# Retention's values and gates: half of their K blocks by seven products in place of eight

## The chip, the cores and the metric

The kernel runs on one core of one Trainium2 chip. The metric is the device time of one execution in microseconds (us). Engines are named as in the profile: PE is TensorE's matmuls, PEld its weight loads, DVE VectorE, ACT ScalarE, POOL GpSimd, SP SyncE, which issues most loads.

## The reference

Two layers of a decoder trunk on 256 positions of width 2048, in float32. Layer 0 mixes with a gated delta rule and latent attention, layer 1 with retention; each layer then has a gated feed-forward network (FFN) with a short convolution and a gated per-layer embedding. The change touches the retention mixer, cut here to what matters:

```python
def odd_mixer(hn, cos, sin, w_in, ret_norm, w_out):
    q, k, v, g = split_cols(hn @ w_in, L1_SPLITS)      # 8 heads: q, k 256 wide, v, g 512 wide
    y = retention(q, k, v, cos, sin, ret_norm)
    return (jax.nn.silu(g) * y) @ w_out

h = h + odd_mixer(rmsnorm(h, attn_norm), ...)
h = h + conv_ffn(rmsnorm(h, ffn_norm), ...)
h = h + ple_term(h, p[1], ...)
```

`retention` rotates q and k, forms per head the decayed scores of q and k, multiplies them by v, and normalises each row of 512 by its mean and variance.

## The kernel before

**Arithmetic.** The 256 rows are two halves of 128 (`NH` = 2). Every float32 operand x is split into hi, a cast to fp32r on ACT, and lo = x - hi on DVE. A product is three matmuls: hi·hi, lo(activation)·hi(weight) and hi·lo(weight). Weights come by SP as 1 MB loads into four `raw` buffers; `cut` (L187, L188) splits them in two pieces of 128x1024 each, into four buffers for hi and four for lo. One load, its two splits and their matmuls are a *unit*: two generator steps for the hi matmuls, one for the lo ones (`UNIT` = 3).

**The two forms of a projection.** `gemm_b` (L266 hi, L271 lo) gives the transposed result, with weights as the stationary operand: 16 matmuls of 512 columns and 16 of 256. `gemm_a` (L295, L296 hi, L301 lo) gives rows of positions: 24 matmuls of 512 columns for four K blocks and 512 output columns.

**Products by sevens.** The FFN's down projection takes part of its K blocks as 2x2 blocks of 512x512 by 512x512 and forms them by seven products instead of eight (`seven`, L442, L443 hi, L447 lo: 12 matmuls each). The activations' four combinations come from `Forms` (L380 to L388). On the weights' side a running total of blocks is kept in two buffers: SP loads the first block into it (`begin`, L407), and POOL's queue issues loads that add the next block to it in memory (`plus`, L411). One operand, t3, is a sum that DVE makes (L467). The seven results are added to h on DVE. The FFN issues one product after each main unit.

**A retention head** (`ret_head`) runs its stages one behind the other: q and k by `gemm_b`, two units each, with rotation on DVE; the values by `gemm_a` over all 16 K blocks, four units, with the scores (L1232) behind the first unit's hi matmuls; then the split of the values (vh L1242 on ACT, vl L1243 on DVE), and the gates by `gemm_a`, four units, with the attention (`mm3`, L244, L245, L247: nine matmuls) behind the first unit's hi matmuls. Statistics (L1258 to L1262, with a reciprocal root on POOL, L156) and normalising (L1265) follow on DVE. `finish` (silu L1272, gate L1273, then the transposes L315 and their split L319, L320 in `gained`) is put off by `later`: it runs as the step of a queue that `turn` serves after each generator step, here the next head's. After heads 3, 5 and 7 the output projection takes up what is ready (`ret_out`, `proj_add`).

**Order.** A list scheduler of the framework orders each engine's instructions from the program's order and its own estimates; each engine then runs its own list strictly in order, and buffers come free as their last readers pass.

Of the kernel before, what the change touches and what calls it, by code (L numbers as in the profile page):

```python
# [13 lines left out]
F32 = mybir.dt.float32  # L14
# [70 lines left out]
def trunk(ctx: ExitStack, tc: tile.TileContext, a: dict):  # L85
# [237 lines left out]

    class Norm:
        def __init__(self, gain):
            self.gain = gain
            self.tiles = []
            self.ssq = small(8)
            self.r = None

        def feed(self, c):
            self.tiles += gained([h[i][c] for i in range(NH)], self.gain + c * 4)
            self.squares(c)
# [12 lines left out]
        def diagonal(self):  # L346
            self.dg = t1((P, 2, P))
            V.tensor_tensor(self.dg, bcm(ident, 2), bcs(self.r, P), op=ALU.mult)
# [20 lines left out]
    class Forms:  # L369
# [6 lines left out]
        def add(self, y0, y1):  # L376
# [4 lines left out]
            V.scalar_tensor_tensor(s2, s1, -1.0, a11, op0=ALU.mult, op1=ALU.subtract)  # L381
            V.tensor_sub(s3, a11, a21)
            V.scalar_tensor_tensor(s4, a12, -1.0, s2, op0=ALU.mult, op1=ALU.subtract)
            hi = [t2((P, 2, 2, P), F32R) for _ in range(2)]
            lo = [t2((P, 2, 2, P), F32R) for _ in range(2)]
            for j in range(2):
                A.copy(hi[j], f[j])
                V.tensor_sub(lo[j], f[j], hi[j].bitcast(F32))  # L388
            self.hi.append(hi)
            self.lo.append(lo)  # L390

        def left(self, n):
            def at(q, k):
                return self.hi[q][n // 2][:, n % 2, k], self.lo[q][n // 2][:, n % 2, k]
            return at

    class Quads:


        def __init__(self, w, r0, c, total):  # L400
            self.blocks = w[r0 : r0 + 8 * P, c * 512 : (c + 2) * 512].rearrange("(q h k p) (e n) -> q h e p k n", q=2, h=2, k=2, e=2)
            self.c = c
            self.total = total

        def put(self, dst, hh, e):
            for q in range(2):
                nc.sync.dma_start(dst[q], self.blocks[q, hh, e])  # L407

        def plus(self, hh, e):
            for q in range(2):  # L410
                G.dma_start(self.total[q], self.blocks[q, hh, e], accum_op=ALU.add)  # L411
# [10 lines left out]
    def running():  # L422
        return [xtile().bitcast(F32).rearrange("p a b c -> p a (b c)") for _ in range(2)]

    def seven(ready, tiles, forms, then):

        quads = ready.popleft()
        c, run_t, fresh, plus = quads.c, quads.total, quads.fresh, quads.plus

        def x(half, i):  # L430
            def at(q, k):
                return xl(tiles, 4 * q + 2 * half + k, i)
            return at

        def product(o, left, right, start):
            los = []
            for q in range(2):
                hi, lo = cut(right[q], 2, 512)
                los.append(lo)
                for k in range(2):  # L440
                    l = left(q, k)
                    T.matmul(o, l[0], hi[k], start=start and q + k == 0, stop=False, skip_group_check=True)  # L442
                    last_mm[0] = T.matmul(o, l[1], hi[k], start=False, stop=False, skip_group_check=True)  # L443
                yield
            for q in range(2):
                for k in range(2):
                    last_mm[0] = T.matmul(o, left(q, k)[0], los[q][k], start=False, stop=q + k == 2, skip_group_check=True)  # L447
            yield

        h11, h12, h21, h22 = h[0][c], h[0][c + 1], h[1][c], h[1][c + 1]  # L450
        acc = pb()
        yield from product(acc, x(0, 0), run_t, True)
        V.tensor_add(h11, h11, acc)
        plus(0, 1)
        one = pb()
        yield from product(one, x(1, 0), fresh(1, 0), True)
        V.tensor_add(h11, h11, one)
        two = pb()
        yield from product(two, forms.left(0), run_t, True)
        V.tensor_sub(h22, h22, two)  # L460
        plus(1, 1)
        b22 = fresh(1, 1)
        yield from product(two, forms.left(3), b22, False)
        V.tensor_sub(h12, h12, two)
        t3 = fresh(0, 1)
        for q in range(2):
            V.tensor_add(t3[q], t3[q], b22[q])  # L467
        yield from product(acc, forms.left(1), run_t, False)
        V.tensor_sub(h12, h12, acc)
        plus(1, 0)  # L470
        yield from product(acc, forms.left(2), t3, False)
        V.tensor_sub(h22, h22, acc)
        yield from product(acc, x(1, 1), run_t, False)
        then()
        V.tensor_add(h21, h21, acc)
# [576 lines left out]
    def ffn(l, nf, nxt, aside=None):  # L1052
# [44 lines left out]
        jobs = deque((g0, c) for g0, cols in by_seven.items() for c in cols)  # L1097
        ready = deque()
        total = []

        def following():
            if not total:
                total.extend(running())
            if jobs:
                g0, c = jobs.popleft()
                ready.append(Quads(w_dn, g0 * P, c, total))
                ready[-1].begin()

        def down(g0, g1, tiles, forms):
            fast = chain(*[seven(ready, tiles, forms, following) for _ in by_seven[g0]])  # L1110
# [13 lines left out]
        for n, (g0, g1) in enumerate(groups):  # L1124
# [3 lines left out]
            for _ in range(LAG * UNIT):  # L1128
                next(going)
            if prev is None:  # L1130
                following()
                run(going)
            else:
                behind_it = down(*prev)
                share = sum(7 if c in by_seven[prev[0]] else 2 for c in range(0, CG, 2)) + 2 * (len(by_seven[prev[0]]) == 1)
                share /= 2 * (g1 - g0) - LAG
                owed = 0.0
                for m, _ in enumerate(going, 1):
                    if m % UNIT:
                        continue  # L1140
                    owed += share
                    while owed >= 1.0:
                        owed -= 1.0
                        for _ in range(UNIT):
                            next(behind_it, None)
                run(behind_it)
# [49 lines left out]
    n1 = Norm(C_NORM["l1_attn_norm"])  # L1196
# [21 lines left out]
    def ret_head(i8, tail):  # L1218
        gq = ret_rope(256 * i8)
        if tail is not None:  # L1220
            later(lambda: None, tail)
        q = run(gq)
        k = run(ret_rope(2048 + 256 * i8))
        dec = t2((P, 384))
        nc.scalar.dma_start(dec, a["decay"][:, 384 * i8 : 384 * (i8 + 1)])
        gv = gemm_a(w1, 0, KB, 4096 + 512 * i8, 512, X1)
        for _ in range(2):
            next(gv)
        ps = pb()
# [7 lines left out]
        ps = run(gv)  # L1237
        v = []
        for i in range(NH):
            vh, vl = t2(dt=F32R), t2(dt=F32R)  # L1240
            r = n1.r[:, i : i + 1]
            A.activation(vh, ps[:, i], AF.Copy, scale=r)  # L1242
            V.scalar_tensor_tensor(vl, ps[:, i], r, vh.bitcast(F32), op0=ALU.mult, op1=ALU.subtract)  # L1243
            v.append((vh, vl))
        gg = gemm_a(w1, 0, KB, 8192 + 512 * i8, 512, X1)
        for _ in range(2):
            next(gg)
        ps = [pb() for _ in range(NH)]
# [4 lines left out]
        mm3(ps[0], [(pl(0), v[0])], True, True)  # L1253
        mm3(ps[1], [(pl(P), v[0]), (pl(S), v[1])], True, True)
        ys = []
        for i in range(NH):
            st = small(6)
            V.bn_stats(st, ps[i])  # L1258
            mv = small(2)
            V.bn_aggr(mv, st)  # L1260
            rs = small(2)
            V.tensor_scalar(rs[:, 0:1], mv[:, 1:2], EPS, None, op0=ALU.add)  # L1262
            rsqrt(rs[:, 1:2], rs[:, 0:1], 1)
            y = t2()
            V.tensor_scalar(y, ps[i], mv[:, 0:1], rs[:, 1:2], op0=ALU.subtract, op1=ALU.mult)  # L1265
            ys.append(y)
        ps = run(gg)

        def finish():
            for i in range(NH):  # L1270
                t = t2()
                A.activation(t, ps[:, i], AF.Silu, scale=n1.r[:, i : i + 1])  # L1272
                V.tensor_mul(ys[i], ys[i], t)  # L1273
            ret_x.extend(gained(ys, C_RN + 4 * i8))

        return finish
# [6 lines left out]
    tail = None  # L1283
# [4 lines left out]
    later(lambda: None, tail)  # L1288
# [204 lines left out]
```

## Time and profile before

| | before |
|---|---|
| three runs | 2855.48, 2854.13, 2855.10 us (median 2855.1) |
| profiled execution | 2853.73 us, its span 2852.0 us |
| granted TensorE clock | 0.999 |
| retention stage | about 1300 to 2060 us of the span |
| loads from memory | 580.94 MB, 204 GB/s over the span |

In the profile's groups, a line such as `L188 DVE ...` gives busy time and mean duration, then the idle time of the engine ahead of it and who ended that. In a timeline a row has its start, its duration, engine, line, operation and tiles; a matmul's listed duration is longer than the step from one start to the next, because they are pipelined, so the step is what counts.

### The profile page before, as it was taken

The numbers are of one execution on the slowest core, as the hardware profiler recorded it, in microseconds if no ns is written. First come the engines' busy times: TensorE is split into PE (matmuls) and PEld (weight loads), VectorE is DVE, ScalarE is ACT, GpSimd is POOL, SyncE is SP. The second block draws the span as 40 slices with busy tenths as digits, with TensorE's granted clock in tenths as the row PEclk, the third lists the DMA queues.
The fourth block names the chain that finished last, engine by engine and source line by source line (L and its number), as shares of the span: only waits on it lengthen the run. The fifth ranks groups of instructions, "written<-read, shape, count | busy, mean of one in ns | idle before, by whom it ended". The sixth has DMA issues, their size and how long they took to land.

```text
span 2852.0 us, 38914 instructions
## 1 busy us (share of the span) xinstructions
PE 2832.8 (99%) x14956; PEld 2440.3 (86%) x14956; DVE 2163.5 (76%) x3016; ACT 1606.0 (56%) x2253; POOL 194.6 (7%) x176
## 2 busy tenths in 40 slices
PE   9999999999999999999999999999999999999998
PEld 9899988888888888888888888888888888888887
DVE  7888867898989898756556565565679899989775
ACT  7666655566666665554444443444556666666554
POOL 0111100011111110000000000000001111111100
PEclk9999999999999999999999999999999999999999
DMA  7444456588888988655555555555559889898854
GB/s 244 131 133 130 131 169 210 187 232 252 244 251 243 255 239 254 189 183 190 182 185 186 188 186 180 192 182 186 193 185 243 254 238 259 236 260 252 242 176 144
DMA packets 422650, 585.57 MB, mean 205 GB/s; under 512 B 12096, under 2 KB 268224, under 8 KB 422464
## 3 DMA queue, kind: packets, MB, share of 16 engines
q1 hardware_dynamic: 389664, 521.66, 55.5%
q0 software_dynamic: 29376, 56.63, 11.8%
q10 hardware_dynamic: 3424, 4.79, 0.5%
q8 instruction: 117, 1.92, 0.3%
q14 instruction: 69, 0.57, 0.1%
HBM read 580.94 MB, written 2.10 MB: 204 GB/s over the span
## 4 chain that ended last, share of the span: by engine, by line
PE 98%; DVE 1%; ACT 1%; DMA 0%; issue 0%; POOL 0%; ACTq 0%; POOLq 0%; DVEq 0%
PE pa L266 30%; PE pa L271 16%; PE pa L301 10%; PE pa L296 10%; PE pa L295 10%; PE pb L443 4%; PE pb L442 4%; PE pb L447 4%; PE pb L735 2%; PE pb L315 1%; PE pb L296 1%; PE pb L295 1%; PE pb L301 1%; PE pa L932 1%; PE pb L741 0%; PE pb L1232 0%
## 5 line engine op out<-in xcount | busy, mean ns | idle before, releaser
L188 DVE TENSOR_TENSOR lo<-raw,hi 128x1024 fp32r<-128x1024 f32 (+3 forms) x1104 | 1153.7, 1069 | 473.7 <-ACT hi L187 399.9
L187 ACT CAST hi<-raw 128x1024 fp32r<-128x1024 f32 (+3 forms) x1104 | 971.2, 927 | 816.6 <-PE pa L296 328.9
L266 PE MATMUL pa<-xg,hi 128*128 128x512 f32 x3840 | 925.5, 391 | 0.0
L266 PEld LDWEIGHTS pa<-xg,hi 128*128 128x128 f32 x3840 | 711.4, 188 | 142.2 <-DVE xg L320 0.3
L271 PEld LDWEIGHTS pa<-xg,lo 128*128 128x128 f32 x3840 | 490.3, 191 | 16.3
L271 PE MATMUL pa<-xg,lo 128*128 128x256 f32 x3840 | 502.0, 283 | 0.0
L295 PE MATMUL pa<-hi,xg 128*128 128x512 f32 (+1 forms) x1284 | 497.6, 388 | 2.0 <-ACT hi L187 1.9
L296 PE MATMUL pa<-hi,xg 128*128 128x512 f32 (+1 forms) x1284 | 495.6, 386 | 1.7 <-DVE xg L479 1.4
L301 PE MATMUL pa<-lo,xg 128*128 128x512 f32 (+1 forms) x1284 | 315.8, 386 | 0.0
L295 PEld LDWEIGHTS pa<-hi,xg 128*128 128x128 f32 x1284 | 241.2, 188 | 48.6 <-ACT hi L187 2.2
L296 PEld LDWEIGHTS pa<-hi,xg 128*128 128x128 f32 x1284 | 241.2, 188 | 48.2 <-DVE xg L479 2.3
L301 PEld LDWEIGHTS pa<-lo,xg 128*128 128x128 f32 x1284 | 238.1, 188 | 45.3
L411 POOL DMA_DIRECT2D xg<-in_l_ffn_w_down_dram x108 | 130.7, 1225 | 1187.1 <-DVE lo L188 795.8
L188 DVE TENSOR_TENSOR lo<-xg,hi 128x1024 fp32r<-128x1024 f32 x144 | 173.8, 1218 | 14.5 <-ACT hi L187 14.1
L187 ACT CAST hi<-xg 128x1024 fp32r<-128x1024 f32 x144 | 146.7, 1050 | 58.1 <-PE pb L443 29.9
L1070 DVE SCALAR_TENSOR_TENSOR t<-t,fp,t 128x255 f32<-128x255 f32 (+1 forms) x352 | 150.3, 477 | 24.7 <-ACT t L1068 24.0
L278 ACT COPY t<-pa 128x512 f32<-128x512 f32 x128 | 75.0, 586 | 82.3 <-PE pa L271 73.0
L1068 ACT ACTIVATE t<-t,fp 128x256 f32<-128x256 f32 x176 | 96.2, 594 | 37.0 <-DVE t L281 37.0
L156 POOL TENSOR_TENSOR small<-small,mhalf 128x1 f32<-128x1 f32 (+2 forms) x38 | 28.8, 757 | 1288.7 <-DVE small L1262 622.6
L443 PE MATMUL pb<-hi,t 128*128 128x512 f32 x288 | 113.1, 393 | 0.0
L442 PE MATMUL pb<-hi,t 128*128 128x512 f32 x288 | 113.0, 392 | 0.0
L279 DVE TENSOR_TENSOR t<-t,pa 128x512 f32<-128x512 f32 x128 | 86.9, 679 | 1.1 <-ACT t L278 1.1
(278 smaller groups left out, 2413.5 us busy)
## 6 DMA issues: line engine op xcount, KB each, us to landing
raw<-in_l_ffn_w_up_dram SPq DMA_DIRECT2D x176, 1024.0 KB, 5.4
raw<-in_l_w_in_dram SPq DMA_DIRECT2D x128, 1024.0 KB, 5.2
raw<-in_l_ffn_w_down_dram SPq DMA_DIRECT2D x108, 512.0 KB, 5.6
xg<-in_l_ffn_w_down_dram POOLq DMA_DIRECT2D x108, 512.0 KB, 6.9
raw<-in_l_w_out_dram SPq DMA_DIRECT2D x44, 1024.0 KB, 5.2
raw<-in_l_ple_gate_dram SPq DMA_DIRECT2D x32, 1024.0 KB, 5.2
xg<-in_l_ffn_w_down_dram SPq DMA_DIRECT2D x36, 512.0 KB, 6.9
raw<-in_l_ffn_w_down_dram SPq DMA_DIRECT2D x16, 1024.0 KB, 5.7
```

The lines of the kernel that those rows point to most:

```text
L187: last_cast[0] = A.copy(vo(hi)[:, c], vi(rk)[:, c])
L188: last_diff[0] = V.tensor_sub(vo(lo)[:, c], vi(rk)[:, c], vo(hi)[:, c].bitcast(F32))
L266: last_mm[0] = T.matmul(ps[:, j], wh, x2, start=first, stop=False)
L271: last_mm[0] = T.matmul(ps[:, j, :S], lo[k][:, j * P : (j + 1) * P], xr(tiles, c * 8 + k)[1], start=False, stop=c == 1 and k == 7)
L295: T.matmul(o[i], xh, hi[k], start=begin and k0 + k == 0, stop=False)
L296: last_mm[0] = T.matmul(o[i], xw, hi[k], start=False, stop=False)
L301: last_mm[0] = T.matmul(o[i], xl(tiles, k0 + k, i)[0], lo[k], start=False, stop=end and k0 + k == nkb - 1)
L411: G.dma_start(self.total[q], self.blocks[q, hh, e], accum_op=ALU.add)
L442: T.matmul(o, l[0], hi[k], start=start and q + k == 0, stop=False, skip_group_check=True)
L443: last_mm[0] = T.matmul(o, l[1], hi[k], start=False, stop=False, skip_group_check=True)
L447: last_mm[0] = T.matmul(o, left(q, k)[0], los[q][k], start=False, stop=q + k == 2, skip_group_check=True)
L1070: V.scalar_tensor_tensor(y[:, j, lag:], u[:, j, : S - lag], fc(ct + (2 - lag) * 88), y[:, j, lag:], op0=ALU.mult, op1=ALU.add)
```

## The change

In each retention head the first 1024 rows of the weights (K blocks 0 to 7) for the values and for the gates together form one 2x2 group, with the two halves of the positions as its rows and values and gates as its columns. `seven` forms it by seven products, one beside each main unit. The main units of a head are now two for q, two for k, two for the values and two for the gates (K blocks 8 to 15 only). The results go to new tiles (`into_new`): the first to arrive is copied by ACT, the later ones are added by DVE, and so are the sums of the plain halves. Values and gates are therefore complete only when a head's last product is, and the split of the values, the attention, the gate and the transposes all move into the next head's first units (`ret_rest`, served by `later`); after heads 3, 5 and 7 into the output projection. In head 0 the products start two units late at a higher rate.

The activations' combinations for this group are made where the norm is fed, in layer 0's gated embedding (`gained_apart`, for the first two column groups). The running total's bookkeeping becomes a class, `Sevens`, used by the FFN too, whose order of products is unchanged.

```diff
+    def gained_apart(src, gain):
...
+            y = t2((P, 2, S))
+            for kk in range(2):
+                A.activation(y[:, kk], ps[:, kk * S : (kk + 1) * S], AF.Copy, scale=col(gain + k2 * 2 + kk))
+            tiles.append(xtile())
+            put_split(tiles[-1], 0, 2, y)
...
         def feed(self, c):
+            if self.forms is not None and c < 2:
+                tiles, whole = gained_apart(src, self.gain + c * 4)
+                self.forms.add(*whole, narrow=c == 0)
...
+    def beside(main, side, lag, share):
...
+            if n % UNIT == 0 and n > lag * UNIT:
+                owed += share
+                while owed >= 1.0:
+                    owed -= 1.0
+                    for _ in range(UNIT):
+                        next(side, None)
...
+    def into_new(cells):
+
+        def put(i, e, src, minus=False):
+            if (i, e) in cells:
+                V.tensor_tensor(cells[i, e], cells[i, e], src, op=ALU.subtract if minus else ALU.add)
+            else:
+                cells[i, e] = t2()
+                A.activation(cells[i, e], src, AF.Copy, scale=-1.0 if minus else 1.0)
+        return put
...
         yield from product(acc, x(1, 1), run_t, False)
-        then()
-        V.tensor_add(h21, h21, acc)
+        sevens.following()
+        put(1, 0, acc)
...
-        gv = gemm_a(w1, 0, KB, 4096 + 512 * i8, 512, X1)
+        gv = gemm_a(w1, 1024, 8, 4096 + 512 * i8, 512, X1[4:])
...
+        for e in range(2):
+            if e == 1:
+                gv = gemm_a(w1, 1024, 8, 8192 + 512 * i8, 512, X1[4:])
+            ps = yield from gv
+            for i in range(NH):
+                put(i, e, ps[:, i])
+        return pt
...
+        def gate():
+            for i in range(NH):
+                t = cells[i, 1]
+                A.activation(t, t, AF.Silu, scale=n1.r[:, i : i + 1])
+                V.tensor_mul(ys[i], ys[i], t)
...
+        return attend, lambda: None, gate, lambda: None, finish
...
     for i8 in range(HEADS):
-        tail = ret_head(i8, tail)
+        cells = {}
+        put = into_new(cells)
+        side = ret_side(put)
+        pt = beside(ret_main(i8, put), side, 2 if i8 == 0 else 0, 7 / 6 if i8 == 0 else 1.0)
+        run(side)
+        later(lambda: None, *ret_rest(i8, cells, pt))
```

What moves on the engines is shown at three places, the first two for head 2. Line numbers of after differ: statistics L1318, L1320, L1322, normalising L1325, gate L1332, vl L1306, additions of results L490, t3 L539, products L513, L514, L519; L188, L266, L271, L315 and L320 keep theirs.

On PE, around the transposes (L315) of y (`t_2396`, `t_2400` in before; `t_2489`, `t_2493` now) in before:

```order
L266 MATMUL pa_13815<-xg_11847,hi_13822 128x512 x2
L266 MATMUL pa_13815<-xg_11857,hi_13822 128x512 x2
L315 MATMUL pb_13849<-ident,t_2396_13694 128x128
L315 MATMUL pb_13849<-ident,t_2400_13703 128x128
L315 MATMUL pb_13849<-ident,t_2396_13694 128x128
L315 MATMUL pb_13849<-ident,t_2400_13703 128x128
L315 MATMUL pb_13859<-ident,t_2396_13694 128x128
L315 MATMUL pb_13859<-ident,t_2400_13703 128x128
L315 MATMUL pb_13859<-ident,t_2396_13694 128x128
L315 MATMUL pb_13859<-ident,t_2400_13703 128x128
L271 MATMUL pa_13815<-xg_11658,lo_13819 128x256 x2
```

and now, from the last matmuls of the next head's first product:

```order
L519 MATMUL pb_14021<-lo_14035,xg_11879 128x512 x2
L315 MATMUL pb_14047<-ident,t_2489_13994 128x128
L315 MATMUL pb_14057<-ident,t_2489_13994 128x128
L266 MATMUL pa_13949<-xg_12076,hi_14068 128x512 x2
L266 MATMUL pa_13949<-xg_12086,hi_14068 128x512 x2
L266 MATMUL pa_13949<-xg_12266,hi_14072 128x512 x2
L266 MATMUL pa_13949<-xg_12276,hi_14072 128x512 x2
L266 MATMUL pa_13949<-xg_12076,hi_14068 128x512 x2
L315 MATMUL pb_14047<-ident,t_2493_14003 128x128
L315 MATMUL pb_14047<-ident,t_2489_13994 128x128
L315 MATMUL pb_14047<-ident,t_2493_14003 128x128
L315 MATMUL pb_14057<-ident,t_2493_14003 128x128
```

In before they stood in a row of eight, in the next head's first unit and three gate units behind the attention (L244 to L247). Now the attention itself stands in that first unit, with 16 matmuls of L271 and one product behind it; two transposes follow, ten matmuls of the second unit (L266), and the other six.

On DVE, from the second half's statistics to the transposes' split (L320), in before:

```order
L1262 TENSOR_SCALAR small_13700<-small_13698 128x1
L1265 TENSOR_SCALAR t_2400_13703<-pb_13677,small_13698,small_13700 128x512
L188 TENSOR_TENSOR lo_13784<-raw_13781,hi_13783 128x1024
L188 TENSOR_TENSOR lo_13788<-raw_13781,hi_13787 128x1024
L188 TENSOR_TENSOR lo_13819<-raw_13816,hi_13818 128x1024
L188 TENSOR_TENSOR lo_13823<-raw_13816,hi_13822 128x1024
L188 TENSOR_TENSOR lo_13887<-raw_13884,hi_13886 128x1024
L1273 TENSOR_TENSOR t_2396_13694<-t_2396_13694,t_2422_13842 128x512
L1273 TENSOR_TENSOR t_2400_13703<-t_2400_13703,t_2423_13845 128x512
L188 TENSOR_TENSOR lo_13891<-raw_13884,hi_13890 128x1024
L320 SCALAR_TENSOR_TENSOR xg_13848<-pb_13849,par,xg_13848 128x256
```

and now:

```order
L1318 BN_STATS small_13996<-pb_13977 128x6
L1332 TENSOR_TENSOR t_2489_13994<-t_2489_13994,t_2443_13759 128x512
L1320 BN_AGGR small_13998<-small_13996 128x2
L188 TENSOR_TENSOR lo_14069<-raw_14066,hi_14068 128x1024
L1322 TENSOR_SCALAR small_14000<-small_13998 128x1
L188 TENSOR_TENSOR lo_14073<-raw_14066,hi_14072 128x1024
L1325 TENSOR_SCALAR t_2493_14003<-pb_13977,small_13998,small_14000 128x512
L188 TENSOR_TENSOR lo_14117<-raw_14113,hi_14116 128x1024
L1332 TENSOR_TENSOR t_2493_14003<-t_2493_14003,t_2425_13677 128x512
L188 TENSOR_TENSOR lo_14125<-raw_14113,hi_14124 128x1024
L320 SCALAR_TENSOR_TENSOR xg_14046<-pb_14047,par,xg_14046 128x256
L320 SCALAR_TENSOR_TENSOR xg_14056<-pb_14057,par,xg_14056 128x256
```

In before five splits of weights (L188) lay between the second half's normalising and the gates (L1273), which waited for the gate projection to end. Now the first gate (L1332) stands between the two halves' steps, and three splits are threaded through the second half's chain.

On DVE, around the split of head 0's values (vl: L1243 in before, L1306 now), in before:

```order
L188 TENSOR_TENSOR lo_12583<-raw_12580,hi_12582 128x1024
L188 TENSOR_TENSOR lo_12587<-raw_12580,hi_12586 128x1024
L188 TENSOR_TENSOR lo_12646<-raw_12643,hi_12645 128x1024
L1243 SCALAR_TENSOR_TENSOR t_2198_12572<-pa_12424,small_12269,t_2197_12571 128x512
L188 TENSOR_TENSOR lo_12650<-raw_12643,hi_12649 128x1024
L1243 SCALAR_TENSOR_TENSOR t_2200_12576<-pa_12424,small_12269,t_2199_12575 128x512
L1258 BN_STATS small_12617<-pb_12606 128x6
L1260 BN_AGGR small_12619<-small_12617 128x2
```

and now, where `xg_12369` and `xg_12370` are the running total's two buffers and `raw_12802` holds the next head's first weights:

```order
L188 TENSOR_TENSOR lo_12769<-xg_12369,hi_12768 128x1024
L188 TENSOR_TENSOR lo_12777<-xg_12370,hi_12776 128x1024
L490 TENSOR_TENSOR t_2239_12683<-t_2239_12683,pa_12648 128x512
L188 TENSOR_TENSOR lo_12805<-raw_12802,hi_12804 128x1024
L490 TENSOR_TENSOR t_2226_12618<-t_2226_12618,pb_12416 128x512
L188 TENSOR_TENSOR lo_12809<-raw_12802,hi_12808 128x1024
L490 TENSOR_TENSOR t_2226_12618<-t_2226_12618,pa_12648 128x512
L188 TENSOR_TENSOR lo_12875<-xg_12369,hi_12874 128x1024
L490 TENSOR_TENSOR t_2232_12646<-t_2232_12646,pb_12416 128x512
L188 TENSOR_TENSOR lo_12887<-xg_12370,hi_12886 128x1024
L1318 BN_STATS small_12839<-pb_12828 128x6
L1306 SCALAR_TENSOR_TENSOR t_2261_12798<-t_2232_12646,small_12309,t_2260_12797 128x512
```

In before both vl stood behind the values' last splits (`raw_12580`), with splits of the gates' weights between them. Now the second vl waits behind the splits of the next group's first block (`lo_12875`, `lo_12887`), which must have been loaded into the buffers that `lo_12769` and `lo_12777` were still read from.

More of the change, by code (lines that the diff above doesn't have):

```diff
@@ L420, in fresh, with __init__, following, into_h @@
             return dst
[L422 to L428, printed above, removed]
+    class Sevens:
+        def __init__(self, w, jobs):
+            self.w = w
+            self.jobs = deque(jobs)
+            self.total = [xtile().bitcast(F32).rearrange("p a b c -> p a (b c)") for _ in range(2)]
+            self.following()
+        def following(self):
+            if self.jobs:
+                self.quads = Quads(self.w, *self.jobs.popleft(), self.total)
+                self.quads.begin()
+    def beside(main, side, lag, share):
+        n, owed = 0, 0.0
+        while True:
+            try:
+                next(main)
+            except StopIteration as e:
+                return e.value
+            n += 1
+            if n % UNIT == 0 and n > lag * UNIT:
[4 more added lines that the diff above has]
+                        next(side, None)
+    def into_h(c):
+        def put(i, e, src, minus=False):
+            V.tensor_tensor(h[i][c + e], h[i][c + e], src, op=ALU.subtract if minus else ALU.add)
+        return put
+    def into_new(cells):
+        def put(i, e, src, minus=False):
+            if (i, e) in cells:
+                V.tensor_tensor(cells[i, e], cells[i, e], src, op=ALU.subtract if minus else ALU.add)
+            else:
+                cells[i, e] = t2()
+                A.activation(cells[i, e], src, AF.Copy, scale=-1.0 if minus else 1.0)
+        return put
+    def seven(sevens, tiles, forms, put):
+        quads = sevens.quads
+        run_t, fresh, plus = quads.total, quads.fresh, quads.plus
         def x(half, i):
@@ L456, in seven @@
         yield from product(one, x(1, 0), fresh(1, 0), True)
-        V.tensor_add(h11, h11, one)
+        put(0, 0, one)
         two = pb()
         yield from product(two, forms.left(0), run_t, True)
-        V.tensor_sub(h22, h22, two)
+        put(1, 1, two, True)
         plus(1, 1)
@@ L463, in seven @@
         yield from product(two, forms.left(3), b22, False)
-        V.tensor_sub(h12, h12, two)
+        put(0, 1, two, True)
         t3 = fresh(0, 1)
@@ L1096, in ffn @@
         by_seven = {g0: [0, 2] if n < len(groups) - 2 else [0] for n, (g0, g1) in enumerate(groups[:-1])}
[L1097 to L1107, printed above, removed]
+        sevens = []
         def down(g0, g1, tiles, forms):
-            fast = chain(*[seven(ready, tiles, forms, following) for _ in by_seven[g0]])
+            fast = chain(*[seven(sevens[0], tiles, forms, into_h(c)) for c in by_seven[g0]])
             rest = [c for c in range(CG) if c - c % 2 not in by_seven[g0]]
```

149 lines of the change are left out of this document (76 added, 73 removed).

## The prediction

> **What bounds the kernel now.** I read the page's totals first, then the chain of waits, then busy times by stretch.
>
> ```profile
> span 2852.0 us, 38914 instructions
> PE 2832.8 (99%) x14956; PEld 2440.3 (86%) x14956; DVE 2163.5 (76%) x3016; ACT 1606.0 (56%) x2253; POOL 194.6 (7%) x176
> PE 98%; DVE 1%; ACT 1%; DMA 0%; issue 0%; POOL 0%; ACTq 0%; POOLq 0%; DVEq 0%
> ```
>
> TensorE is busy for 99% of the span and holds 98% of the chain that ended last. So time can only go where matmuls go, and time can only come where TensorE has to wait for another engine. The profiled execution took 2853.73 us: its span of 2852.0 and 1.7 around it. The median of the three runs is 2855.1, 1.4 more; I do the sum on the profiled execution and add 1.4 at the end.
>
> The change works in the retention stage. Busy times by stretch, columns: stretch, its length, then busy time and instructions of PE, PEld, DVE, ACT, POOL, the granted clock, the DMA share and GB/s. The first row is one turn of the second layer's FFN (a main unit plus a product), the second is one retention head, the third is 400 us of that FFN.
>
> ```profile
> 2310.46:2318.74 8.28, 8.28 (x45) 7.17 (x44) 8.28 (x14) 5.16 (x7) 0.00 (x0) 1.00 0.82 266
> 1369.40:1439.57 70.17, 70.17 (x346) 59.36 (x346) 42.05 (x53) 30.04 (x36) 1.09 (x2) 1.00 0.54 177
> 2160.00:2560.00 400.00, 400.00 (x2138) 346.71 (x2138) 360.37 (x458) 251.22 (x301) 45.99 (x38) 1.00 0.89 248
> ```
>
> A head takes 70.17 us, PE is busy in all of it, the clock is full, and DVE (60%) and ACT (43%) have room. The third row matters as a precedent: the FFN already runs products by sevens between its units, with DVE at 90%, DMA at 0.89 and 248 GB/s, and PE still never waits.
>
> **What it removes.** In each of 8 heads, 1024 of the 2048 rows of both projections (values, gates) are now one 2x2 group of seven products instead of eight. The rows are the starts of matmuls in the timeline: first a plain unit of 24 matmuls, then a main unit alone, then a main unit and a product.
>
> ```profile
> 1328.14 0.39 PE L295 MATMUL pa<-hi,xg 128*128 128x512 f32 x1
> ...
> 1331.76 1.98 PE L301 MATMUL pa<-lo,xg 128*128 128x512 f32 x8
> 1333.58 0.39 PE L295 MATMUL pa<-hi,xg 128*128 128x512 f32 x1
> ```
>
> ```profile
> 1882.86 3.82 PE L266 MATMUL pa<-xg,hi 128*128 128x512 f32 x16
> 1886.51 2.08 PE L271 MATMUL pa<-xg,lo 128*128 128x256 f32 x16
> 1888.42 1.78 PE L266 MATMUL pa<-xg,hi 128*128 128x512 f32 x7
> ...
> 2302.17 3.79 PE L266 MATMUL pa<-xg,hi 128*128 128x512 f32 x16
> 2305.80 2.08 PE L271 MATMUL pa<-xg,lo 128*128 128x256 f32 x16
> 2307.71 0.40 PE L442 MATMUL pb<-hi,t 128*128 128x512 f32 x1
> ...
> 2310.46 3.79 PE L266 MATMUL pa<-xg,hi 128*128 128x512 f32 x16
> ```
>
> From 1328.14 to 1333.58 are 24 matmuls: 5.44 us, 0.2267 each. A main unit alone takes 1888.42-1882.86 = 5.56. The turn in the FFN from 2302.17 to 2310.46 takes 8.29, so a product of 12 matmuls costs 2.72 (12 x 0.2267 gives the same). Per head four plain units go, 4 x 5.44 = 21.76, and seven products come, 7 x 2.72 = 19.04. That is 2.72 per head and **21.8 us** in eight heads: 96 matmuls, which is the whole difference on TensorE. Without any wait the profiled execution would be 2853.7 - 21.8 = 2831.9.
>
> The Trainium skill, page "TensorE: Matmul & The Clock Gate", section "Back-to-back issue gap", gives about 131 ns per matmul of 512 columns in a sustained stream and some 216 ns for a single one. By the first figure 96 matmuls would be worth an estimated 12.6 us, by the second 20.7. The 24 rows above are a sustained stream at 227 ns, so this case's trace contradicts the first and lies near the second; I keep the trace.
>
> **What it adds off TensorE.** Mean durations by form (busy us, mean ns, in the retention window), and the splitting of a weight piece:
>
> ```profile
> L188 DVE TENSOR_TENSOR lo<-raw,hi 128x1024 fp32r<-128x1024 f32 x174 | 209.8, 1220 | 121.3 <-ACT hi L187 115.9 <-PE pa L271 2.4 <-PE pa L301 2.2
> L467 DVE TENSOR_TENSOR raw<-raw,raw 128x1024 f32<-128x1024 f32 x4 | 4.8, 1219 | 3.5 <-DMA raw<-in_l_ffn_w_down_dram 3.5
> L453 DVE TENSOR_TENSOR t<-t,pb 128x512 f32<-128x512 f32 x2 | 1.4, 679 | 0.0
> L187 ACT CAST hi<-raw 128x1024 fp32r<-128x1024 f32 x176 | 177.6, 1049 | 190.7 <-PE pa L296 101.5 <-PE pa L266 49.0 <-issue 33.8
> L387 ACT CAST t<-t 128x512 fp32r<-128x512 f32 x6 | 3.5, 617 | 0.2 <-DVE t L381 0.2
> ```
>
> Seven products have 14 pieces to split where the four units had 8: six more on DVE (7.3) and ACT (6.3), two additions for the t3 operand (2.4), about seven additions of results (4.8) on DVE, and four first copies on ACT (near 2.5). DVE goes from 42.05 to 56.6 us in a head of 67.45 (84%), ACT to 38.8 (58%), loads from 12 to 15 MB per head (about 230 GB/s). All three lie below the FFN's row (90%, 63%, 248), so averages hide it. What remains are single places where a chain is long and its cover short.
>
> **Place 1: the transposes behind the attention.** Before, statistics, normalising and gate lie a whole projection ahead of the transposes. Now the same chain, with the split of two or three weight pieces queued between its steps, must be through when TensorE reaches the six transposes in the next head's second unit. The rows of the attention of head 0 in before:
>
> ```profile
> 1343.10 0.39 PE L247 MATMUL pb<-t,t 128*128 128x512 f32 x1
> ...
> 1344.47 0.15 DVE L1262 TENSOR_SCALAR small<-small 128x1 f32<-128x1 f32 x1
> 1344.68 1.98 PE L301 MATMUL pa<-lo,xg 128*128 128x512 f32 x8
> ...
> 1345.36 0.81 DVE L1265 TENSOR_SCALAR t<-pb,small,small 128x512 f32<-128x512 f32 x1 [0.73 <-POOL small L156]
> 1346.09 0.69 DVE L1258 BATCH_NORM_STATS2 small<-pb 128x6 f32<-128x512 f32 x1
> ...
> 1346.69 1.21 DVE L188 TENSOR_TENSOR lo<-raw,hi 128x1024 fp32r<-128x1024 f32 x1
> ...
> 1874.50 1.03 PE L315 MATMUL pb<-ident,t 128*128 128x128 f32 x8
> 1875.29 0.96 PE L271 MATMUL pa<-xg,lo 128*128 128x256 f32 x6
> ```
>
> ```profile
> L1273 DVE TENSOR_TENSOR t<-t,t 128x512 f32<-128x512 f32 x6 | 3.9, 686 | 0.0
> L1265 DVE TENSOR_SCALAR t<-pb,small,small 128x512 f32<-128x512 f32 x4 | 3.2, 810 | 2.8 <-POOL small L156 2.8
> L1260 DVE BATCH_NORM_AGGREGATE small<-small 128x2 f32<-128x6 f32 x4 | 0.7, 180 | 0.1
> ```
>
> DVE: from the third attention matmul (1343.10) to the second statistics (1346.09) 2.99 us. Then statistics 0.69, gate 0.69, aggregate 0.18, a split 1.22, 0.15, a split 1.22, normalise 0.81, a split 1.22, gate 0.69: 6.87 by sums, 6.16 if each neighbour overlaps by the 0.09 seen here (1346.69 starts that much before the listed end of 1346.09+0.69). So 9.15 to 9.86. TensorE: the remaining attention 1344.68-1343.10 = 1.58, 16 short matmuls 2307.71-2305.80 = 1.91, a product 2.72, two transposes 0.2 (1875.29-1874.50 over 8), ten matmuls of the unit 10 x 0.228 = 2.28: 8.69. So TensorE waits 0.46 to 1.17; I take 0.75, a little under the middle. The attentions of heads 1, 2, 4 and 6 have this form: **3.0 us** (0 if DVE runs ahead, 4.7 at most). Behind heads 3, 5 and 7 stands the out-projection: 1.58, eight lo matmuls 1.81 and a whole unit 5.44 make 8.83, against a DVE chain with one split fewer, 8.64 at most. Nothing waits there.
>
> **Place 2: the seam from head 0 to head 1.** Head 0 starts its products two units late, so its seventh product falls into head 1's first unit. Only after its lo split may the load for the next running total start, and DVE has that total's two splits queued ahead of the second values' lo part (vl), which the attention's seventh matmul needs. The rows: a product's last split and the matmuls that use it in the FFN, then the landing of such loads (line 407) and its median for the running total alone:
>
> ```profile
> 2314.27 1.22 DVE L188 TENSOR_TENSOR lo<-xg,hi 128x1024 fp32r<-128x1024 f32 x1
> ...
> 2317.84 1.07 PE L447 MATMUL pb<-lo,xg 128*128 128x512 f32 x4
> ...
> L407 SPq DMA_DIRECT2D raw<-in_l_ffn_w_down_dram x108: 367/368/1092, 567.6 to 2677.9; - x108
> DMA to landing us min/median/max: 3.8/5.7/9.9
> ...
> xg<-in_l_ffn_w_down_dram SPq DMA_DIRECT2D x36, 512.0 KB, 6.9
> ```
>
> The chain is landing 6.9, cast 1.05, split 1.22, an addition 0.68, split 1.22, statistics 0.70, vl 0.75: 12.5. TensorE covers it with the rest of the product (two matmuls), eight matmuls of the unit, six of the attention and eight short ones, 0.45+1.82+1.36+0.96 = 4.6, plus the lead that a split has over TensorE, in the FFN 2317.84-2315.49 = 2.4. So it waits 5.5; leads vary and I take **5.0** (2 with the shortest landing, 9 with 9.9). From vl on, DVE still has aggregate 0.18, the step over POOL 1345.36-1344.47 = 0.89, normalise 0.81, statistics 0.69, gate 0.69, and the rest of place 1's chain (5.49): 8.75, or 8.0 with the overlaps. TensorE has 0.68+0.96+2.72+0.2+2.28 = 6.8 before the transposes: another **1.5** (0 to 1.9). Both happen once.
>
> **Place 3: small ones.** The feed of the retention's norm in the first layer's gated embedding now makes combined forms twice: per feed some four 512-wide operations more on DVE and on ACT, 4 x 0.68 = 2.7 us. A stretch of that stage (columns as above):
>
> ```profile
> 1262.00:1300.00 38.00, 38.00 (x185) 31.93 (x184) 23.74 (x32) 21.88 (x34) 0.70 (x1) 1.00 0.62 201
> ```
>
> DVE is busy for 62%, so a unit of 5.44 us leaves it 2.0, and two units cover a feed; I put **0.5** (0 to 5.4 if none is covered). The rope tables move to an earlier stretch, where nothing that TensorE waits for is shown: 0, 1 either way.
>
> **Sum:** 2853.7 - 21.8 + 3.0 + 5.0 + 1.5 + 0.5 = 2841.9 for a profiled execution, and with 1.4 a median of **2843**.
>
> **The rivals.**
> - *No waits at all.* As the FFN's row shows PE at 400.00 of 400.00 with the same product and a busier DVE, DVE may run far enough ahead. Then 2855.1 - 21.8 = 2833.3. Against: places 1 and 2 are chains with short cover, which the FFN has not got. 0.15.
> - *The t3 operand comes late, and it gets slower.* Its load gets a buffer only when the third unit's weights are split. From the head's start that unit's lo matmuls begin after two turns of 8.29, 2.84 of attention and transposes and 3.65 of the unit: 23.1; the split is done some 2 us sooner, at 21.1. Landing 5.7, the addition on t3 (1.22), which stands in DVE's order ahead of the fourth unit's lo split, and that split (1.22): 29.2. TensorE needs it one turn later, at 31.4. The margin is 2.1 us. With the longest landing of that line, 9.9, TensorE is 2.1 us late in each head: 2843 + 17 = 2860. It decides at 1.5 us per head (12 us of net gain over eight), a landing of 9.3 in every head; with 11.8, the longest of the accumulating loads, it would be 2875. For it: DVE sat idle before that addition 10 times of 36 in the FFN. Against: TensorE did not wait once for what followed. 0.04.
>
> ```profile
>   DMA raw<-in_l_ffn_w_down_dram: 24.8, 10
> ...
> DMA to landing us min/median/max: 5.8/6.9/11.8
> ```
>
> - *All chains at their long ends:* 4.7 + 9 + 1.9 + 5.4 = 21.0, which gives nearly everything back: 2854, within 0.2%. A part of it, 12 to 17 us, is likelier: 2846 to 2850, in the range below. 0.05 for the whole.
> - *The removed matmuls are worth less than the pitch.* If the weight load beside each were what paces, 2440.3/14956 = 0.163 us, 96 would bring 15.7 and the median would be 2855.1 - 15.7 + 10 = 2849. Against: PEld is busy for 86% and PE for 99%, and no row shows a stream faster than 0.2267. The 131 ns of the Trainium skill's page "TensorE: Matmul & The Clock Gate" would point the same way. 0.01.
> - *It does not do what it says* is excluded: the program has exactly 96 fewer matmuls.
>
> **How the numbers follow.** 0.75 for the forecast's form (a part of the gain eaten by waits), the rest as above. The range runs from no waits, 2833, to 18 us of waits, 2851; the late t3 and a full loss lie outside it. Faster, within, slower go by 0.2%, 5.7 us, about what a measurement of this kernel can tell from no change: 0.90 (the first two cases), 0.06 (long ends, pitch), 0.04.
>
> **What would show it.** The matmul count falls by 96 and the head's period from 70.17 to about 68.2 in heads 1, 2, 4, 6 and 67.5 in heads 3, 5. The waits show TensorE at L315 for DVE, 0.75 us four times, and at the attention for vl, about 5 us once. DVE in a head is near 84%. It is wrong if PE waits at the fourth unit's L271 for lo (t3 late), at L513 for hi (the running total late), or if the product's pitch differs from 0.2267.

## The result, and the profile after

| | before | after |
|---|---|---|
| runs | 2854.13 to 2855.48 us, median 2855.11 of 4 | 2840.12 to 2840.59 us, median 2840.22 of 4 |
| profiled execution | 2853.73, span 2852.0 | 2840.12, span 2838.4 |
| ratio of the times | | 0.9949, 95% interval 0.9931 to 0.9966 |

The changed kernel is 14.9 us faster; the forecast was 12 (2843). By their times all four executions of after, and three of the four of before, are some 1.4 us longer through a stretch of half clock near 32 us (last section), so the 14.9 compares like with like. The first rows of the page of after, as those of before in the prediction:

```profile
span 2838.4 us, 39187 instructions
PE 2814.4 (99%) x14860; PEld 2423.0 (85%) x14860; DVE 2271.4 (80%) x3146; ACT 1674.4 (59%) x2343; POOL 259.9 (9%) x224
PE 96%; DVE 1%; issue 1%; ACT 1%; DMA 0%; POOL 0%; ACTq 0%; POOLq 0%; SPq 0%; DVEq 0%
```

TensorE has 14860 matmuls, 96 fewer, and is still the bound, but its share of the chain fell from 98% to 96%: something waits now. The stretches from one head's attention to the next, in after (columns as in the prediction):

```profile
1363.63:1432.22 68.59, 67.79 (x335) 56.94 (x334) 56.13 (x69) 38.65 (x47) 10.47 (x9) 1.00 0.85 237
1432.22:1500.78 68.56, 67.76 (x334) 56.98 (x333) 54.89 (x67) 37.87 (x46) 9.25 (x8) 1.00 0.84 233
```

A head takes 68.56 us instead of 70.17: 1.6 less, not 2.72. DVE is busy for 80 to 82% of it, ACT for 55 to 56% (forecast 84% and 58%), and PE is idle for 0.8. What PE waited for in the whole of after (us in total, times, longest):

```profile
PE pb L315 <- DVE t L1332: 4.0, 5, 0.8
PE pa L295 <- ACT hi L187: 1.9, 1, 1.9
PE pb L801 <- DVE t L920: 1.6, 1, 1.6
PE pa L296 <- DVE xg L551: 1.4, 2, 0.7
```

Only the first row is new; the others stand in before too, under its line numbers:

```profile
PE pa L295 <- ACT hi L187: 1.9, 1, 1.9
PE pb L729 <- DVE t L848: 1.6, 1, 1.6
PE pa L296 <- DVE xg L479: 1.4, 2, 0.7
```

There are five waits at the transposes (L315) for the second half's gate (L1332): behind heads 0, 1, 2, 4 and 6. Behind heads 3, 5 and 7 there is none, as forecast. Nothing waits at the attention, at the products or at the plain units' lo parts. The timeline of after around one of the five, behind head 1:

```profile
1439.06 2.54 PE L266 MATMUL pa<-xg,hi 128*128 128x512 f32 x10
...
1439.80 0.81 DVE L1325 TENSOR_SCALAR t<-pb,small,small 128x512 f32<-128x512 f32 x1 [0.45 <-POOL small L156]
1440.53 1.22 DVE L188 TENSOR_TENSOR lo<-raw,hi 128x1024 fp32r<-128x1024 f32 x1
1441.66 0.68 DVE L1332 TENSOR_TENSOR t<-t,t 128x512 f32<-128x512 f32 x1
...
1442.40 0.88 PE L315 MATMUL pb<-ident,t 128*128 128x128 f32 x6 [0.80 <-DVE t L1332]
```

The last of the ten matmuls starts at 1439.06 + 2.54 - 0.39 = 1441.21, and at a step of 0.227 us the next instruction could have started at 1441.44. The transposes start at 1442.40, 0.06 after the gate's end: 0.96 us late (the waits view shows 0.8, as it counts from a matmul's listed end). DVE itself waited 0.45 for POOL's root in that chain, which the forecast had hidden behind a weight split. The rows of the two halves' roots show why the split did not hide it:

```profile
1434.36 0.56 POOL L156 TENSOR_TENSOR small<-small,mhalf 128x1 f32<-128x1 f32 x1 [0.90 <-DVE small L1322]
...
1438.14 1.21 DVE L188 TENSOR_TENSOR lo<-raw,hi 128x1024 fp32r<-128x1024 f32 x1
...
1438.30 1.46 POOL L156 TENSOR_TENSOR small<-small,mhalf 128x1 f32<-128x1 f32 x1 [3.39 <-DVE small L1322]
```

The first half's root runs while DVE is idle and takes 0.56 us; the second half's runs beside the split and takes 1.46, to 0.41 behind the split's end. It is so in all eight heads (0.56 to 0.57 and 1.40 to 1.46). In before DVE is idle beside all 16 roots, and each takes 0.54 to 0.56. (The profile's spans on POOL are rough, but DVE's wait of 0.45 fits them.)

### The profile page after: what moved, and what is told of

Its sections match the earlier page's. It is cut to its first block, busy times and chain, and to the rows that moved or that the text cites. A ratio compares the mean times of both kernels' runs of the same rounds, so it can differ in the third digit from the quotient of the medians.

```text
span 2838.4 us, 39187 instructions
## 1 busy us (share of the span) xinstructions
PE 2814.4 (99%) x14860; PEld 2423.0 (85%) x14860; DVE 2271.4 (80%) x3146; ACT 1674.4 (59%) x2343; POOL 259.9 (9%) x224
## 4 chain that ended last, share of the span: by engine, by line
PE 96%; DVE 1%; issue 1%; ACT 1%; DMA 0%; POOL 0%; ACTq 0%; POOLq 0%; SPq 0%; DVEq 0%
PE pa L266 30%; PE pa L271 16%; PE pa L301 8%; PE pa L296 8%; PE pa L295 8%; PE pb L514 6%; PE pb L513 6%; PE pb L519 6%; PE pb L807 2%; PE pb L315 1%; PE pb L296 1%; PE pb L295 1%; PE pb L301 1%; PE pa L1004 1%; PE pb L813 0%
## 5 line engine op out<-in xcount | busy, mean ns | idle before, releaser
L188 DVE TENSOR_TENSOR lo<-raw,hi 128x1024 fp32r<-128x1024 f32 (+3 forms) x1088 | 1135.9, 1068 | 356.0 <-ACT hi L187 280.5
L187 ACT CAST hi<-raw 128x1024 fp32r<-128x1024 f32 (+3 forms) x1088 | 956.0, 926 | 691.0 <-PE pa L266 221.0
L266 PE MATMUL pa<-xg,hi 128*128 128x512 f32 x3840 | 926.9, 392 | 0.0
L266 PEld LDWEIGHTS pa<-xg,hi 128*128 128x128 f32 x3840 | 712.1, 188 | 142.8 <-DVE xg L320 0.3
L271 PEld LDWEIGHTS pa<-xg,lo 128*128 128x128 f32 x3840 | 490.9, 191 | 16.9
L271 PE MATMUL pa<-xg,lo 128*128 128x256 f32 x3840 | 501.6, 283 | 0.0
L295 PE MATMUL pa<-hi,xg 128*128 128x512 f32 (+1 forms) x1028 | 399.0, 388 | 2.0 <-ACT hi L187 1.9
L296 PE MATMUL pa<-hi,xg 128*128 128x512 f32 (+1 forms) x1028 | 396.7, 386 | 1.7 <-DVE xg L551 1.4
L188 DVE TENSOR_TENSOR lo<-xg,hi 128x1024 fp32r<-128x1024 f32 x208 | 252.0, 1220 | 30.8 <-ACT hi L187 30.3
L187 ACT CAST hi<-xg 128x1024 fp32r<-128x1024 f32 x208 | 211.8, 1050 | 87.6 <-PE pb L514 50.2
L301 PE MATMUL pa<-lo,xg 128*128 128x512 f32 (+1 forms) x1028 | 252.5, 386 | 0.0
L295 PEld LDWEIGHTS pa<-hi,xg 128*128 128x128 f32 x1028 | 193.7, 188 | 38.7 <-ACT hi L187 2.2
L296 PEld LDWEIGHTS pa<-hi,xg 128*128 128x128 f32 x1028 | 193.7, 188 | 38.4 <-DVE xg L551 2.3
L301 PEld LDWEIGHTS pa<-lo,xg 128*128 128x128 f32 x1028 | 190.3, 188 | 35.6
L514 PE MATMUL pb<-hi,t 128*128 128x512 f32 x416 | 163.1, 392 | 0.0
L513 PE MATMUL pb<-hi,t 128*128 128x512 f32 x416 | 163.0, 392 | 0.0
L514 PE MATMUL pb<-hi,xg 128*128 128x512 f32 x312 | 122.4, 392 | 0.0
L513 PE MATMUL pb<-hi,xg 128*128 128x512 f32 x312 | 122.3, 392 | 0.0
```

The source lines that it names most:

```text
L187: last_cast[0] = A.copy(vo(hi)[:, c], vi(rk)[:, c])
L188: last_diff[0] = V.tensor_sub(vo(lo)[:, c], vi(rk)[:, c], vo(hi)[:, c].bitcast(F32))
L266: last_mm[0] = T.matmul(ps[:, j], wh, x2, start=first, stop=False)
L271: last_mm[0] = T.matmul(ps[:, j, :S], lo[k][:, j * P : (j + 1) * P], xr(tiles, c * 8 + k)[1], start=False, stop=c == 1 and k == 7)
L295: T.matmul(o[i], xh, hi[k], start=begin and k0 + k == 0, stop=False)
L296: last_mm[0] = T.matmul(o[i], xw, hi[k], start=False, stop=False)
```

## The experiments

Each edit is to the changed kernel unless it says otherwise.

### The transposes two turns later

```diff
-        return attend, lambda: None, gate, lambda: None, finish
+        return attend, lambda: None, gate, lambda: None, lambda: None, lambda: None, finish
```

> The transposes of a head are put two turns later, behind all 16 hi matmuls of the next head's second unit instead of in the middle of them; nothing else changes. Theory A (what eats the gain is TensorE's wait at those transposes, 0.96 us in each of five heads): 2840.2 - 4.8 = 2835.4 us, and no wait of PE at L315 for DVE L1332. Theory B (DVE and ACT are simply at their limit, and the wait comes back at the next place, at lo or hi of a later unit): 2840 within 0.5 us, with the wait under another line.

Measured: 2833.65 us median (2832.91 to 2835.36), ratio to before 0.9928 (0.9912 to 0.9945). The profiled executions of after and of this kernel both have the half clock: 2840.12 and 2834.07, 6.0 apart. The timeline of this kernel at the place shown above, behind head 1, and PE's three largest waits:

```profile
1437.74 3.80 PE L266 MATMUL pa<-xg,hi 128*128 128x512 f32 x16
...
1440.48 0.69 DVE L1332 TENSOR_TENSOR t<-t,t 128x512 f32<-128x512 f32 x1
...
1441.38 1.04 PE L315 MATMUL pb<-ident,t 128*128 128x128 f32 x8
...
1442.17 2.16 PE L271 MATMUL pa<-xg,lo 128*128 128x256 f32 x16
```

```profile
PE pa L295 <- ACT hi L187: 1.9, 1, 1.9
PE pb L801 <- DVE t L920: 1.6, 1, 1.6
PE pa L296 <- DVE xg L551: 1.4, 2, 0.7
```

The gate now ends at 1441.17, 0.2 us ahead of the transposes, and no wait of PE is left in the retention stage. Theory A holds, B falls: the wait did not come back elsewhere. The stretch from head 1's attention to head 2's in this kernel:

```profile
1431.04:1498.48 67.44, 67.44 (x334) 57.10 (x333) 54.63 (x67) 37.85 (x46) 9.25 (x8) 1.00 0.85 237
```

A head takes 67.44 us, as 70.17 - 2.72 = 67.45 says without any wait, and 1.12 less than in after. Of the 1.12 the wait is 0.96; the other 0.16 goes with the transposes standing in one row instead of two, and was not traced further. Five times 1.12 are 5.6 us; the rest of the 6.0 lies within what single executions differ by.

### One turn later

```diff
-        return attend, lambda: None, gate, lambda: None, finish
+        return attend, lambda: None, gate, lambda: None, lambda: None, finish
```

> The transposes' step comes one turn later. In TensorE's order the first two transposes move behind eight matmuls of the unit, but the other six keep their place behind ten (twelve behind head 0). Theory A (what costs is only where the six stand, against the second half's gate on DVE): no change, 2840.2, five waits of some 0.8 us at L315. Theory B (the step was simply too early in the turns): about half of what two turns gave, 2837.

Measured: 2839.47 us median (2838.02 to 2840.27), PE's waits at L315 4.0 us in five, as in after. Half of what two turns gave would have been 2837; it is theory A, with the profiled execution, which has the half clock, at 2840.27 beside after's 2840.12. The turn in which a step is issued only says when it may start earliest. Where the transposes stand is set by the list scheduler, and it kept six of the eight where they were.

### The chain shorter, and longer

```diff
             for i in range(NH):
                 t = cells[i, 1]
                 A.activation(t, t, AF.Silu, scale=n1.r[:, i : i + 1])
-                V.tensor_mul(ys[i], ys[i], t)
+                if i == 0:
+                    V.tensor_mul(ys[i], ys[i], t)
```

> Leaves out the second half's multiplication by its gate (rows 128 to 255 of the retention's output go ungated), which shortens the DVE chain ahead of the six transposes by one operation of 0.6 us; the list scheduler answers by putting the six transposes eight matmuls (1.8 us) earlier and one weight split behind the chain's end. Theory A (the wait is what the scheduler's estimate of DVE lacks; it moves the transposes to wherever it believes the chain ends): waits stay near 0.8 to 1.2 us five times, total 2840 within 1 us. Theory B (the wait is the chain's length against a given cover): 0.6 us less in each of five heads, 2837.

Measured: 2838.98 us median (2838.01 to 2839.57), of which the profiled one, without the half clock, took 2838.01.

```diff
                 V.tensor_mul(ys[i], ys[i], t)
+                if i == 1:
+                    V.tensor_scalar(ys[i], ys[i], 1.0, None, op0=ALU.mult)
```

> Adds a multiplication by 1.0 to the second half's gated values, 0.6 us more in the DVE chain, with one weight split (1.1 us) now ahead of it too; the list scheduler answers by putting the six transposes behind all 16 matmuls, 1.4 us later. Theory A (as above): the wait becomes 0.96 + 1.7 - 1.4 = 1.3 us in four heads, total 2842 within 1. Theory B (chain's length against a given cover): 1.7 us more in each of five heads, 2848.

Measured: 2839.79 us median (2839.36 to 2841.20), the profiled one, without the half clock, 2839.36. PE's first wait in the kernel with the second gate left out:

```profile
PE pb L315 <- DVE t L1325: 4.2, 5, 0.9
```

and in the one with the longer chain:

```profile
PE pb L315 <- DVE t L1334: 4.3, 5, 0.9
```

A shorter chain and a longer one leave the same five waits, 4.2 and 4.3 us against 4.0, each for the operation that now ends the chain. Theory B falls in both: without the half clock it gives 2835.5 and 2846.5. Theory A holds in kind; for the longer chain its 1.3 us in four heads and 2842 (2840.5 without the half clock) were too high. So the scheduler puts the six transposes where it believes the chain will end (behind two, ten or sixteen matmuls of the unit in the three kernels), and on the chip the chain ends about a microsecond later than that. That its estimate is what falls short is inferred from these three orders; the estimates are not on record. Putting the step two turns later kept the transposes behind the true end. What part of the chain the scheduler underrates was not tried either. DVE's wait for POOL's root, 0.45 in the rows above and 0.44 to 0.46 in all three kernels, would be half of it if the scheduler reckons with the 0.56 us that the root takes beside an idle DVE.

### Half of the heads plain

```diff
-        gv = gemm_a(w1, 1024, 8, 4096 + 512 * i8, 512, X1[4:])
+        r0, nk, tiles = (1024, 8, X1[4:]) if i8 < 4 else (0, KB, X1)
+        gv = gemm_a(w1, r0, nk, 4096 + 512 * i8, 512, tiles)
...
-        side = ret_side(put)
+        side = ret_side(put) if i8 < 4 else iter(())
```

(and the same for the gates; the list of groups ends after head 3; transposes two turns later.)

> As finish_two_later, but heads 4 to 7 multiply all 16 K blocks of values and gates plainly: 48 matmuls of 512 columns come back. Theory A (each removed matmul is worth TensorE's pitch of 0.2267 us): 10.9 us over finish_two_later, 2846.3 if that takes 2835.4. Theory B (it is worth the weight load's 0.163 us, the products being paced otherwise): 7.8 over it, 2843.2. Theory C (products also cost DVE time that TensorE waits for, beside the transposes): less than 10 us over it.

Measured: 2845.26 us median (2843.92 to 2845.84). Without the half clock: 2843.92 and 2843.94 here, 2832.91 and 2833.22 in the kernel with the transposes two turns later, 10.9 apart in the mean (10.7 to 11.0 by pairs). Theory A: 48 matmuls at 0.2267 are 10.9. Theories B and C fall: seven products in four heads take no more of TensorE's time than their matmuls, and DVE's 13 to 14 us of extra work per head cost nothing once the transposes are out of the way.

### The first loads' order

```diff
         def diagonal(self):
-            self.dg = t2((P, 2, P))
+            self.dg = (t1 if self.forms is None else t2)((P, 2, P))
```

> The changed kernel with the norms' diagonal in the small tiles again (t1), except for the retention's norm; this puts the load of the positions back to its old place, behind four other loads in SP's queue. Theory A (the half clock of 3.4 us near 32 us hangs on the order of the first loads, and costs 1.5 us): 2840.2 - 1.5 = 2838.7, granted clock full near 32 us. Theory B (that stretch of half clock falls where it likes, whatever the loads' order): 2840.2, clock as in the changed kernel.

Measured: 2838.38 us median (2837.75 to 2840.04). That is theory A's number, but not its reason: one of the four executions, 2840.04, has the half clock by its time, so the order of the loads does not keep it away. And in the kernel before:

```diff
-            self.dg = t1((P, 2, P))
+            self.dg = t2((P, 2, P))
```

> The kernel before with one word changed: the norms' diagonal in the big tiles (t2), as the change has it. Theory A (this alone moves the positions' load ahead and brings the half clock near 32 us): 2855.1 + 1.5 = 2856.6, granted clock 0.5 for some 3.4 us near 32 us. Theory B (the half clock has nothing to do with it): 2855.1, full clock there.

Measured: 2854.79 us median of 10 (2854.21 to 2856.44) beside 2854.25 of 14 for the kernel before (2853.57 to 2855.67); ratio 1.0002 (0.9993 to 1.0012). Executions with and without the half clock occur in both kernels, so it does not hang on this order: theory B. The big tile may still cost something: at a granted clock of 0.999 the medians are 2854.57 (of 6) and 2853.69 (of 8), at 0.998 they are 2855.98 (of 4) and 2855.13 (of 6), 0.9 apart each time, which lies inside the interval. The traces show one place for a part of it, and it is not the first loads. If the matmuls of the other kernels are matched one by one with those of before, all eight with the big tile lose 0.2 to 0.8 us at a row of transposes near 474 us, and the two with the small one lose nothing there. In the kernel before with the big tile this wait reads:

```profile
PE pb L315 <- DVE t L365: 0.2, 1, 0.2
```

With the big tile the retention's rope tables are made at 455 to 457 us, with the small one at 515 to 516. That they are what delays the transposes behind them is not shown.

### Head 0 without its lag

```diff
+        if i8 == 0:
+            start_sevens()
         q = yield from ret_rope(256 * i8)
-        if i8 == 0:
-            start_sevens()
...
-        pt = beside(ret_main(i8, put), side, 2 if i8 == 0 else 0, 7 / 6 if i8 == 0 else 1.0)
+        pt = beside(ret_main(i8, put), side, 0, 1.0)
```

> The changed kernel with head 0 run like the others: its products start behind its first unit at one per unit, so that its seventh product falls into its own last units and not into head 1's first. Theory A (the seam costs nothing in the changed kernel: its load lands in time and the splits run far enough ahead): no change but for the clock, 2838.7 with the clock full near 32 us and 2840.2 without, five waits at L315. Theory B (the seam costs part of what was forecast for it, hidden in lines other than the values' lo part): up to 5 us less, 2835.

Measured: 2838.61 us median (2838.33 to 2839.90), PE's waits at L315 3.9 us in five. The profiled execution, with the half clock, took 2839.90, after's 2840.12. Theory A: the seam costs nothing that can be told.

### The version that beats both

finish_two_later with the small diagonal tiles (both edits above).

> finish_two_later and diagonal_as_before together. Theory A (waits at the transposes are the one loss; the diagonal's place is worth nothing that can be told): 2833.1 in executions with the clock full near 32 us and 2834.6 in those without, as finish_two_later. Theory B (the order of the first loads costs some 0.7 us by itself, as the kernel before with the diagonal moved hints): 2832.4 and 2833.9.

Measured: 2832.66 us median of 5 (2832.63 to 2834.14), ratio to before 0.9923 (0.9910 to 0.9937), beside 2854.15 for the kernel before on the same chip. That is 21.5 of the 21.8 us that the removed matmuls are worth. Three of its five executions took 2832.63 to 2832.66, two of finish_two_later's four 2832.91 and 2833.22; the difference leans to theory B, but the two kernels ran on different chips, and it is too small to be settled.

## Why the prediction was right, and where its parts were wrong

- **The gain, 21.8 us.** Right. Half of it came back as 10.9 with four heads plain, a head without the wait takes the 67.44 us that the sum gives, and the best version gets 21.5 of it by the medians. The rival by the weight loads' pace falls, and with it the 131 ns per matmul that the Trainium skill's page "TensorE: Matmul & The Clock Gate", section "Back-to-back issue gap", gives for a sustained stream: these runs show 227.
- **Place 1, 3.0 us (0.75 in four heads, with head 0 under place 2).** Right in place and kind, small in size: five waits of 0.96 us, 1.1 each with what goes with them, 5.5 in all. The forecast set DVE's 9.15 to 9.86 against TensorE's 8.69 behind the third attention matmul; the gate behind head 1 ended 9.7 after it (1432.22 + 0.45 to 1442.34), and TensorE was ready 8.8 after it. So the sum was sound, and 0.75 was too low a choice from its 0.46 to 1.17: the neighbours do overlap, but POOL's root put 0.45 back. What the working took for a fixed cover is none, though: with a shorter or a longer chain the transposes moved too, and the wait stayed.
- **Place 2, 5.0 + 1.5 us.** Wrong. The failing step is the "landing 6.9" against a lead of 2.4: the sum gave 5.5 of wait, and there was none. The rows of after at the seam: the splits of the seventh product, the running total's load, the last use, the cast of the next total:

```profile
1354.17 2.36 DVE L188 TENSOR_TENSOR lo<-xg,hi 128x1024 fp32r<-128x1024 f32 x2 [2.47 <-ACT hi L187]
...
1355.42 1.50 SPq L436 DMA_DIRECT2D xg<-in_l_w_in_dram  x2
...
1360.21 1.05 ACT L187 CAST hi<-xg 128x1024 fp32r<-128x1024 f32 x1 [0.69 <-PE pb L514]
...
1360.90 1.08 PE L519 MATMUL pb<-lo,xg 128*128 128x512 f32 x4
...
1365.12 0.74 DVE L1306 SCALAR_TENSOR_TENSOR t<-t,small,t 128x512 fp32r<-128x512 f32 x1
...
1365.98 0.43 PE L245 MATMUL pb<-t,t 128*128 128x512 f32 x1
```

The splits were done at 1356.53, 4.4 us ahead of TensorE, not 2.4. The loads landed in 4.2 to 4.4 us, not 6.9, and the cast that followed waited for TensorE to free a hi buffer, not for the data. vl was ready at 1365.86 and TensorE came for it at 1365.98. From the cast on the chain took 5.65 us, as worked out (5.62), and it ended 0.1 us ahead. The forecast had taken both numbers from the FFN, which moves 248 GB/s with DVE at 90%; in the retention stage it is 233 to 237 GB/s with DVE at 80 to 82%. That this is why the landings are shorter is not shown. Head 0's wait at the transposes, forecast here as 1.5, is one of the five of place 1. The landings of line 436 in after, over the whole run and then from 1300 to 2060 us alone:

```profile
DMA to landing us min/median/max: 3.6/5.3/10.5
```

```profile
DMA to landing us min/median/max: 3.6/4.6/6.7
```

- **Place 3, 0.5 us.** No wait appeared in layer 0's gated embedding: 0.
- **The late t3.** Did not happen. DVE's addition L539 has 16 instructions in the retention stage and no idle time before any of them; from 1300 us on, the loads of such operands (line 436 into `raw`) landed within 6 us, where the working had 5.7 and a margin of 2.1, so the margin was never used up.
- **The rope tables, 0 (1 either way).** Right within its bounds: they move from 515 to 457 us, and the transposes near 474 us then lose 0.3 us in after.
- **The sum.** 10 us of waits were forecast, 6.9 came (21.8 - 14.9): the seam's 6.5 and place 3's 0.5 were not there, and place 1 took 2.5 more than its own term. The two profiled executions, 13.6 apart, can be matched matmul by matmul, which places what is missing from 21.8: 1.6 of half clock that only after's has, 0.3 at the transposes near 474 us, 5.5 in the retention stage, and 0.7 behind the last matmul, where the eleven traces differ by as much (10.4 to 11.1 us). That the total came within 3 us is partly luck: 7 us of terms that did not come stood against 4 that were too small or missing.

## What to carry to other kernels

Where a scheduler orders by its own estimates, a wait of constant size behind a chain points at the estimates: here a longer and a shorter chain moved the waiting instruction along, and issuing it two turns later removed the wait. Landings and leads are better taken from the stage that is being changed than from another that already has the operation: here they differed by 2.6 and 2.0 us. Where one engine's stream is the bound, count its instructions times their pitch first: here that gave the gain to a few tenths, and everything else was a list of single places to be checked.

## What the hardware showed besides

Windows of the same 3.4 us in before and in after, columns as above (the third number from the end is the granted clock); before:

```profile
31.97:35.39 3.42, 3.42 (x22) 3.37 (x20) 3.21 (x14) 2.63 (x10) 0.00 (x0) 1.00 0.56 149
28.60:30.40 1.80, 0.00 (x0) 0.00 (x0) 0.00 (x0) 1.72 (x6) 0.00 (x0) 1.00 0.01 5
```

and after:

```profile
31.97:35.39 3.42, 3.42 (x13) 3.24 (x12) 3.21 (x14) 2.73 (x9) 0.00 (x0) 0.50 0.57 164
28.60:30.40 1.80, 0.01 (x1) 0.01 (x1) 0.03 (x1) 1.78 (x6) 0.00 (x0) 1.00 0.02 5
```

Shortly after the start both kernels leave TensorE idle for 1.86 us. In the profiled execution of after the clock was then halved for 3.41 us (13 matmuls instead of 22), which costs 1.5 us; in that of before it was not. It is a matter of the execution, and the eleven traces show what decides it. Five have the halving. The trace records the granted clock by stretches: the half clock lasts 3.413 us each time, and it begins 27.307 us (three) or 23.893 us (two) after the first record of the full clock, which is 8 and 7 times 3.413. If a grid of this step is laid from that record through all eleven traces, the gap of 1.86 us lies in a single window in these five (at least 1.83 us of it, by the matmuls' listed ends), and the halving begins where that window ends. In the other six the gap crosses a border of the grid, with at most 1.73 us in one window, and the clock stays full. So what decides is how the gap lies to the grid, and the share of a window that must be idle is between 1.73 and 1.83 of 3.41 us here. The Trainium skill, page "TensorE: Matmul & The Clock Gate", section "What's actually happening", has the gate watch activity in free-running windows of 3413 ns, which fits the length and the grid; it puts the halving behind a whole idle window, and here 1.83 us of idleness in one were enough.
